# Storing fifteen partitions of two chunks by Pool's software queue, and 112 of the others by the hardware queue

## The chip, the core and the metric

The kernel runs on one core of a Trainium2 chip. The metric is device time in microseconds (us), lower is better; a run of before and of a variant share a chip, and only runs of the fast state are compared. Two variants did not always run on one chip; on every chip used, before took 164.6 to 164.9 us (medians), and where two variants are compared the ratios to before agree with the difference quoted. A profile is one execution, with times counted from the start of its span; its span is about 1.8 us shorter than the device time of the same execution.

## The reference

```python
x_flat = x.reshape(-1, 256)                    # 32768 x 256, fp32
y = x_flat @ W + scale * (((x_flat @ lora_A) * lora_E) @ lora_B)
```

The output is 32768 x 256 in fp32. So 33.6 MB come in and 33.6 MB go out, and the weights are small: `W + A diag(E) B` is folded into one 256 x 256 matrix on the chip.

## The kernel before

The rows are cut into eight chunks of 4096. In a chunk, partition p holds 32 consecutive rows of 256 floats, a *line* of 32 KB that is contiguous in DRAM too. Six "homes" in SBUF (the on-chip memory of 128 partitions) hold chunks; a chunk is loaded, multiplied, its result written over its input, and stored from there. All DMAs are issued by SP on one hardware queue.

```python
ORDER = ["L0", "L1", "L2", "L3", "L4", "L5",
         "S0", "S1", "L6", "L7", "S2", "S3", "S4", "S5", "S6", "S7"]
...
x_chunks = x_flat.rearrange("(c p b) k -> c p b k", p=P, b=ROWS)   # P = 128, ROWS = 32
y_chunks = out_flat.rearrange("(c p b) m -> c p b m", p=P, b=ROWS)
homes = [sbuf(f"home{h}", [P, ROWS, K], FP32) for h in range(N_HOMES)]
...
    else:                                       # a store, in SP's program
        sync.wait_ge(s_chunk, c + 1)
        sync.dma_start(out=y_chunks[c], in_=home(c)[:]).then_inc(...)
...
# the last store stands after the five engines' programs have ended
nc.sync.dma_start(out=y_chunks[last], in_=home(last)[:])
```

Pool (GpSimd) casts x to bf16, TensorE transposes and multiplies, ScalarE and VectorE move results out of PSUM. Pool's program ends with its casts.

## Time and profile before

| | before |
|---|---|
| time, median of 4 runs | 164.65 us (164.32 to 165.16) |
| span of the profile | 163.2 us |
| DMA, mean over the span | 413 GB/s |
| busiest compute engine | PE, 60% |
| last eviction ends (timeline) | 121.8 us |

The slices view cuts the span in 40 equal parts (4.08 us each). Its DMA row is the mean busy share of 16 DMA engines in tenths, and GB/s is what they moved. The queue table gives for each queue its packets, MB and share of 16 engines' span. The windows view gives for a stretch the busy time of each engine, the granted clock, the DMA share and GB/s.

```profile
PE   0399938999999999999920099999950000000000
DMA  5999998998998999999999999999999999999980
GB/s 163 412 458 454 393 506 385 426 474 385 466 434 385 498 401 387 393 474 420 418 466 393 442 450 393 468 426 418 450 418 426 458 401 458 442 401 466 418 385 16
q1 hardware_dynamic: 2944, 67.41, 96.7%
```

The DMA row stands at 8 or 9 tenths from the second slice to the last but one, while the PE row is empty in the last ten slices. The kernel is bound by its DMA engines, and at the end by stores alone.

The trace also has each DMA packet with its start, duration and size, and each engine's completion increment. A 32 KB line is one packet and takes 1213 ns. Followed back from the last increment, the late engine moves eight such lines in each of the last four stores. The sixteen increments of the last store land at 159.30 us (first), 160.08 us (fifteenth) and 162.26 us (sixteenth): one engine is 2.2 us late. Its lines took mostly 1274 to 1300 ns while stores ran beside compute, and 1213 ns in loads and after compute had ended. Its number the trace does not give, and its cause is open.

### The profile page before, as it was taken

The numbers are of one execution on the slowest core, as the hardware profiler recorded it, in microseconds if no ns is written. First come the engines' busy times: TensorE is split into PE (matmuls) and PEld (weight loads), VectorE is DVE, ScalarE is ACT, GpSimd is POOL, SyncE is SP. The second block draws the span as 40 slices with busy tenths as digits, with TensorE's granted clock in tenths as the row PEclk, the third lists the DMA queues.
The fourth block names the chain that finished last, engine by engine and source line by source line (L and its number), as shares of the span: only waits on it lengthen the run. The fifth ranks groups of instructions, "written<-read, shape, count | busy, mean of one in ns | idle before, by whom it ended". The sixth has DMA issues, their size and how long they took to land. (4 is left out here: it accounts for less than half of the span.)

```text
span 163.2 us, 2145 instructions
## 1 busy us (share of the span) xinstructions
PE 98.3 (60%) x778; PEld 81.7 (50%) x778; DVE 79.5 (49%) x66; ACT 66.1 (40%) x65; POOL 67.1 (41%) x70
## 2 busy tenths in 40 slices
PE   0399938999999999999920099999950000000000
PEld 0268827888888888888810078888840000000000
DVE  0116961888888888888850026888870000000000
ACT  3045723767777676767720026676720000000000
POOL 1445516767777677777400256677400000000000
PEclk9999996999999999999995558999995555555555
DMA  5999998998998999999999999999999999999980
GB/s 163 412 458 454 393 506 385 426 474 385 466 434 385 498 401 387 393 474 420 418 466 393 442 450 393 468 426 418 450 418 426 458 401 458 442 401 466 418 385 16
DMA packets 2948, 67.43 MB, mean 413 GB/s; under 512 B 497, under 2 KB 513, under 8 KB 641
## 3 DMA queue, kind: packets, MB, share of 16 engines
q1 hardware_dynamic: 2944, 67.41, 96.7%
q14 instruction: 4, 0.02, 0.0%
HBM read 33.85 MB, written 33.55 MB: 413 GB/s over the span
## 5 line engine op out<-in xcount | busy, mean ns | idle before, releaser
L171 DVE COPY home<-psum_y 128x1024 f32<-128x1024 f32 x64 | 78.4, 1225 | 32.3 <-PE psum_y L192 29.6
L141 POOL CAST stage<-home 128x1024 bf16<-128x1024 f32 x64 | 66.4, 1041 | 48.3 <-DMA home<-in_x_dram 24.5
L152 ACT COPY xt<-psum_xt 128x1024 bf16<-128x1024 bf16 x64 | 64.8, 1012 | 52.2 <-PE psum_xt L184 52.2
L192 PE MATMUL psum_y<-weff,xt 128*128 128x256 bf16 x512 | 69.8, 281 | 0.9
L192 PEld LDWEIGHTS psum_y<-weff,xt 128*128 128x128 bf16 x512 | 47.9, 101 | 14.6 <-issue 7.1
L184 PE MATMUL psum_xt<-ident,stage 128*128 128x128 f32 x260 | 42.0, 287 | 14.5 <-PEq L177 14.5
L184 PEld LDWEIGHTS psum_xt<-ident,stage 128*128 128x128 f32 x260 | 32.7, 149 | 16.6 <-issue 15.6
L204 PE MATMUL psum_y<-ident,a_sb 128*16 128x128 f32 x2 | 0.6, 394 | 6.8 <-DMA a_sb<-in_lora_A_dram 6.8
L157 DVE TENSOR_SCALAR ate<-psum_y,e_sb 16x256 f32<-16x256 f32 x1 | 0.5, 471 | 7.5 <-PE psum_y L204 7.5
L204 PEld LDWEIGHTS psum_y<-ident,a_sb 128*16 128x16 f32 x2 | 0.1, 90 | 6.8 <-issue 6.8
L210 PE MATMUL psum_y<-b_sb,ate 16*128 16x256 f32 x4 | 2.1, 670 | 0.0
L167 DVE TENSOR_TENSOR weff<-w_sb,psum_y 128x512 bf16<-128x512 f32 x1 | 0.7, 689 | 2.4 <-PE psum_y L210 2.4
L152 ACT ACT_TABLE_LOAD x1 | 1.3, 1283 | 0.9 <-SPq L218 0.9
L210 PEld LDWEIGHTS psum_y<-b_sb,ate 16*128 16x128 f32 x4 | 1.2, 319 | 0.5 <-issue 0.3
L123 POOL MEMSET ident<- 128x128 f32 x1 | 0.2, 205 | 0.5 <-SPq L218 0.5
L125 POOL TENSOR_SCALAR_AFFINE_SELECT ident<-ident 128x128 f32<-128x128 f32 x1 | 0.3, 293 | 0.2 <-POOL ident L123 0.2
L246 POOL MEMSET const-float32-0.0<- 128x1 f32 x1 | 0.1, 98 | 0.2 <-issue 0.2
L246 POOL MEMSET const-bfloat16-1.0<- 128x1 bf16 x1 | 0.1, 101 | 0.0
L246 POOL MEMSET const-uint8-127<- 128x1 uint8 x1 | 0.1, 101 | 0.0
L246 POOL MEMSET const-float32-1.0<- 128x1 f32 x1 | 0.1, 98 | 0.0
## 6 DMA issues: line engine op xcount, KB each, us to landing
out_dram<-home SPq DMA_DIRECT2D x8, 4096.0 KB, 42.4
home<-in_x_dram SPq DMA_DIRECT2D x7, 4096.0 KB, 28.5
home<-in_x_dram SPq DMA_DIRECT2D x2, 1024.0 KB, 5.2
home<-in_x_dram SPq DMA_DIRECT2D x1, 2048.0 KB, 10.0
w_sb<-in_W_dram SPq DMA_DIRECT2D x1, 256.0 KB, 5.1
a_sb<-in_lora_A_dram SPq DMA_DIRECT2D x1, 16.0 KB, 4.8
e_sb<-in_lora_E_dram SPq DMA_DIRECT2D x1, 0.1 KB, 4.5
b_sb<-in_lora_B_dram SPq DMA_DIRECT2D x1, 16.0 KB, 3.9
```

The source lines that it names most:

```text
L123: gpsimd.memset(ident[:], 0.0).then_inc(s_ident, 1)
L125: gpsimd.affine_select(out=ident[:], in_=ident[:], compare_op=ALU.not_equal, fill=1.0, base=0, pattern=[[-1, P]], channel_multiplier=1,).t ...
L141: gpsimd.tensor_copy(out=stage[g % NS][:], in_=home(c)[:, b:b + CG, :]).then_inc(s_stage, 1)
L152: scalar.copy(out=xt[g % NX][:], in_=halves).then_inc(s_xt, 1)
L157: vector.tensor_scalar(out=ate[:], in0=psum_y[0][:R, :KT, :P], scalar1=e_sb[:], scalar2=float(scale), op0=ALU.mult, op1=ALU.mult,).then_in ...
L167: vector.tensor_add(out=weff[:], in0=w_sb[:], in1=psum_y[1][:, :KT, :]).then_inc(s_free, NY)
L171: vector.tensor_copy(out=home(c)[:, b:b + CG, :], in_=psum_y[g % NY][:]).then_inc(s_free, 1)
L184: ins = tensor.transpose(psum_xt[i % NT][:, b, :], words[:, b, :], ident[:])
L192: ins = tensor.matmul(psum_y[i % NY][:, b, :], xt[i % NX][:, b, t, :], weff[:, t, :], start=(t == 0), stop=(t == KT - 1),)
L204: ins = tensor.transpose(psum_y[0][:R, t, :P], a_sb[:, t, :], ident[:])
L210: ins = tensor.matmul(psum_y[1][:, t, :], ate[:, t, :], b_sb[:], start=True, stop=True)
L246: nc = _bacc.Bacc("TRN2", target_bir_lowering=False, num_devices=1)
```

## The change

The intent is to give one DMA engine two lines fewer. In chunks 4 and 5, partitions 0 to 111 stay on the hardware queue (by division, seven lines for each of 16 engines). Partitions 112 to 126 send 31 of their 32 rows, for both chunks, by Pool's software queue: fifteen shares of two lines, meant for fifteen engines. Before them, a DMA of five partitions goes out on the same queue; it is meant to turn the choice of engines so that the fifteen leave out the late one. Row 31 of these partitions and all of partition 127 go in small DMAs.

```diff
+PAIR = (4, 5)
+SKIPPED = 4
+COMMON = 112
-    homes = [sbuf(f"home{h}", [P, ROWS, K], FP32) for h in range(N_HOMES)]
+    homes = sbuf("homes", [P, N_HOMES, ROWS, K], FP32)
...
-                sync.dma_start(out=y_chunks[c], in_=home(c)[:]).then_inc(...)
+                if c not in PAIR:
+                    parts = [(slice(P), slice(ROWS))]
+                else:
+                    parts = [
+                        (slice(COMMON + SKIPPED + 1, P - 1), slice(ROWS - 1, ROWS)),
+                        (slice(P - 1, P), slice(0, ROWS, 2)),
+                        (slice(P - 1, P), slice(1, ROWS, 2)),
+                        (slice(COMMON), slice(ROWS)),
+                    ]
+                for i, (p, b) in enumerate(parts):
+                    sync.dma_start(out=y_chunks[c, p, b], in_=home(c)[p, b]).then_inc(...)
...
+        gpsimd.wait_ge(s_chunk, PAIR[1] + 1)      # after Pool's last cast
+        for p, b in (
+            (slice(COMMON, COMMON + SKIPPED + 1), slice(ROWS - 1, ROWS)),
+            (slice(COMMON, P - 1), slice(ROWS - 1)),
+        ):
+            gpsimd.dma_start(out=y_pair[p, :, b], in_=home_pair[p, :, b]).then_inc(s_pair, 16)
+        gpsimd.wait_ge(s_pair, 32)
+        for s in s_rows:
+            gpsimd.wait_ge(s, 16)
```

More of the change, by code (lines that the diff above doesn't have):

```diff
@@ L90 @@
     s_chunk = sem("chunk_done")
+    s_pair = sem("pair_stored")
+    s_rows = [sem(f"rows_stored_{c}") for c in PAIR]
     def home(c):
-        return homes[c % N_HOMES]
+        return homes[:, c % N_HOMES]
     sync, gpsimd, scalar, vector, tensor = nc.sync, nc.gpsimd, nc.scalar, nc.vector, nc.tensor
@@ L119, in sync_program @@
                 sync.wait_ge(s_chunk, c + 1)
-                sync.dma_start(out=y_chunks[c], in_=home(c)[:]).then_inc(stored_of.get(c, stored_rest), 16)
+                if c not in PAIR:
[8 more added lines that the diff above has]
+                for i, (p, b) in enumerate(parts):
+                    done = s_rows[PAIR.index(c)] if len(parts) > 1 and i == 0 else stored_of.get(c, stored_rest)
+                    sync.dma_start(out=y_chunks[c, p, b], in_=home(c)[p, b]).then_inc(done, 16)
     def gpsimd_program():
@@ L144, in gpsimd_program @@
         gpsimd.drain().then_inc(s_stage, 1)
+        gpsimd.wait_ge(s_chunk, PAIR[1] + 1)
+        y_pair = y_chunks[PAIR[0]:PAIR[1] + 1].rearrange("c p b m -> p c b m")
+        home_pair = homes[:, PAIR[0]:PAIR[1] + 1]
+        for p, b in (
[6 more added lines that the diff above has]
+            gpsimd.wait_ge(s, 16)
     def scalar_program():
@@ L228 @@
     last = int(ORDER[-1][1:])
-    nc.sync.dma_start(out=y_chunks[last], in_=home(last)[:])
+    nc.sync.dma_start(out=y_chunks[last], in_=home(last))
 _INS = ['x', 'W', 'lora_A', 'lora_B', 'lora_E', 'scale']
```

## The prediction

> **What bounds the kernel now.** The 16 DMA engines. In the slices view the DMA row stands at 9 tenths from the fourth slice or so to the end, and the queue table gives one hardware queue 96.7% of 16 engines' span (413 GB/s, 163.2 us). No compute engine is over 60% busy; the last eviction ends at 121.8 us, and the last 40 us are stores alone. In the trace's packets a 32 KB line takes 1213 ns; each engine moves 120 (145.6 us) and some smaller ones.
>
> **The uneven end.** The last store's completion increments land at 159.3 to 160.1 us from fifteen engines and at 162.26 us from one. The kernel waits 2.2 us for it alone. Following that engine's packets backwards: its lines took 1274 to 1300 ns between 63 and 82.7 us and between 105 and 120 us, and one took 1865 ns at 100.9 us. There stores run beside compute; in loads, and in stores after compute, it runs at 1213 ns. The trace does not number the engines, so I can't see which it is.
>
> **What the change does.** Chunks 4 and 5 were 16 lines of 32 KB on every engine. Now partitions 0 to 111 go by the hardware queue (14 lines per engine), and partitions 112 to 126 by Pool's queue, two 31 KB lines on each of fifteen engines. Leftover 1 KB rows go in small DMAs. [...]
>
> Costs per engine, with a 1 KB packet at 46 ns and a completion write at 9 ns (trace), and a 31 KB line at 1175 ns (estimate from 1213):
> - fifteen engines: 2 x (1175 - 1213) = -76, 1 KB packets +184 to +276, completions about +75: +0.2 to +0.3 us;
> - the one left out: -2426 + about 350 = -2.1 us.
>
> If that is the late one, it comes in at about 160.2 us, the others at about 160.3: the last landing moves from 162.26 to about 160.4, all on the critical path. Pool's casts end near 118 us, before its DMAs; at S7's issue (122.2 us) three chunks are still queued[...]. Compute and the first 90 us are unchanged.
>
> **Prediction.** 162.9 us (-1.1%), 162.1 to 165.2 in 8 cases of 10. Chances: faster by over 2% 0.04, within 2% 0.92, slower by over 2% 0.04. The floor is near 162.5 us, since the balanced engines still need their 160.
>
> **What would show it.** Right: span near 161.3 us; the last increments within about 1 us; a second queue with about 0.95 MB; total bytes unchanged; the lines of 1274 to 1300 ns still on one engine, which has two lines fewer. Wrong engine: one ends early, near 158 us, and the late one stays, at about 162.5 (time 164.9).
>
> **What would make it wrong.** [...]fifteen partitions are spread otherwise; the slow engine changes between runs or chips; the slowness belongs to the profile; [...]Pool's wait[...] lengthens the end.

+0.2 to +0.3 us for fifteen engines and -2.1 us for the one left out put the last landing at 160.4 us instead of 162.26, and the time at 162.9 us. That the one left out is the late one was assumed. SP's issues take 0.33 to 0.70 us each in the profile before, and three chunks are queued when the last store is issued; that they hide behind the queue was an estimate.

## The result

The changed kernel takes 180.83 us (median of 4 runs, 180.06 to 181.49) against 164.65 us. The ratio is 1.0978, interval 1.0924 to 1.1032: slower by 16 us. Ratios here are the mean time of one kernel's fast runs over that of the other's of the same rounds, so not quite the ratio of the medians quoted.

The slices and the queue table of the changed kernel (a slice is now 4.49 us):

```profile
PE   0499849999999999997009999980000000000000
DMA  5998999999899998998999999999999998999510
GB/s 190 434 485 372 452 467 416 401 467 445 372 467 467 350 432 387 461 459 387 438 459 423 403 452 430 423 424 424 194 256 313 307 285 321 394 438 408 219 73 15
q1 hardware_dynamic: 3080, 66.44, 90.2%
q0 software_dynamic: 80, 0.96, 3.5%
```

The MB are the same in sum (67.4). Compute ends at the same time, as the last two evictions show (VectorE's timeline, before and then after):

```profile
119.20 2.58 DVE L171 COPY home<-psum_y 128x1024 f32<-128x1024 f32 x2 [0.24 <-PE psum_y L192]
```

```profile
119.17 2.58 DVE L204 COPY homes<-psum_y 128x1024 f32<-128x1024 f32 x2 [0.24 <-PE psum_y L225]
```

The DMA row still says 9 tenths, yet from the 29th slice (126 us) the same busy engines move 194 to 321 GB/s instead of some 430. The windows view, before and then after:

```profile
core 0: us, PE busy (x) PEld busy (x) DVE busy (x) ACT busy (x) POOL busy (x), PEclk, DMA share, GB/s
120.00:150.00 30.00, 0.51 (x5) 0.20 (x3) 1.65 (x2) 0.00 (x0) 0.00 (x0) 0.55 1.01 435
```

```profile
120.00:150.00 30.00, 0.49 (x5) 0.19 (x2) 1.62 (x2) 0.00 (x0) 0.00 (x0) 0.55 1.00 296
```

The engines were as busy (1.00) and moved 296 GB/s instead of 435. So nothing waits for a command: the packets themselves take longer. From the packets that start after 115 us:

```
                  32 KB lines: n, mean ns, longest    31 KB lines: n, mean ns, longest
before            578   1213   1293                   -
after             548   1395   5179                   30   3281   8114
```

This accounts for the loss. The 548 lines took 182 ns too long on average, 100 us of engine time; the 30 software lines 2106 ns too long against my estimate of 1175, 63 us. Together that is 163 us on 16 engines, 10.2 us each. The mean of the last store's sixteen increments moved by 10.4 us, from 159.82 to 170.23. The rest is unevenness: the last increment came 8.5 us after that mean (178.74 us), before 2.4 us after it. 10.4 + 6.1 is the 16.5 us between the two last increments.

What the prediction assumed, that the engine left out is the late one, did come true. The trace does not number engines, but on one engine each packet starts 3 to 4 ns before the one ahead of it ends, so an engine can be followed where its packets are alone. Four of the sixteen in the changed kernel, from 104 to 135 us:

```
mean ns of its 32 KB lines    31 KB lines    2 KB packets of the software queue
(104.5 to 119 us)
1213                          2              1
1213                          2              0
1289                          0              1
1213                          2              1
```

The engine with the slow lines is the one that got no 31 KB line. It got a packet of the five-partition DMA. The same holds in three later variants (e5, e11, e14). The right engine was relieved. By what rule the queue chooses its engines no run shows.

One other thing is new: SP waits for Pool before it issues the last store (SP's waits, then SP's timeline, of the changed kernel).

```profile
SPq L251 <- POOLq L251: 19.3, 1, 19.3
```

```profile
141.41 0.35 SPq L262 DMA_DIRECT2D out_dram<-homes  x1
```

### The profile page after: what moved, and what is told of

Read it like the earlier page. It is cut to its first block, busy times and chain, and to the rows that moved or that the text cites. A ratio compares the mean times of both kernels' runs of the same rounds, so it can differ in the third digit from the quotient of the medians.

```text
span 179.7 us, 2155 instructions
## 1 busy us (share of the span) xinstructions
PE 100.6 (56%) x778; PEld 82.7 (46%) x778; DVE 79.5 (44%) x66; ACT 66.1 (37%) x65; POOL 68.3 (38%) x72
## 5 line engine op out<-in xcount | busy, mean ns | idle before, releaser
L204 DVE COPY homes<-psum_y 128x1024 f32<-128x1024 f32 x64 | 78.4, 1225 | 32.2 <-PE psum_y L225 30.2
L163 POOL CAST stage<-homes 128x1024 bf16<-128x1024 f32 x64 | 66.4, 1040 | 48.3 <-PE psum_xt L217 27.0
L225 PE MATMUL psum_y<-weff,xt 128*128 128x256 bf16 x512 | 70.7, 284 | 0.2
L217 PE MATMUL psum_xt<-ident,stage 128*128 128x128 f32 x260 | 42.8, 291 | 12.8 <-PEq L210 12.8
L217 PEld LDWEIGHTS psum_xt<-ident,stage 128*128 128x128 f32 x260 | 33.3, 152 | 15.0 <-issue 14.0
L174 POOL DMA_DIRECT2D out_dram<-homes x2 | 1.2, 626 | 1.2 <-PE psum_xt L217 1.2
```

The lines of the kernel that those rows point to most:

```text
L163: gpsimd.tensor_copy(out=stage[g % NS][:], in_=home(c)[:, b:b + CG, :]).then_inc(s_stage, 1)
L174: gpsimd.dma_start(out=y_pair[p, :, b], in_=home_pair[p, :, b]).then_inc(s_pair, 16)
L204: vector.tensor_copy(out=home(c)[:, b:b + CG, :], in_=psum_y[g % NY][:]).then_inc(s_free, 1)
L217: ins = tensor.transpose(psum_xt[i % NT][:, b, :], words[:, b, :], ident[:])
L225: ins = tensor.matmul(psum_y[i % NY][:, b, :], xt[i % NX][:, b, t, :], weff[:, t, :], start=(t == 0), stop=(t == KT - 1),)
```

## The experiments

**The theories.** *Partitions*: how long a line takes depends on which partitions are read at the same time, not on its size alone. In before's trace every store after 115 us has all 128 partitions, and a 32 KB line takes 1213 ns there, 27.0 GB/s. The change departs from that form twice: the software shares read partitions 112 to 126 alone, and two stores have 112 partitions instead of 128. This was a supposition, to be tested by runs that differ in partitions. The recorded expectations call it theory 1 or the ports theory, after a mechanism; what they say of the mechanism, and the model made from it, is cut, since no run shows it and the trace numbers neither engines nor partitions. The times that they expect stand as estimates. *Rivals*: the software queue, by itself or beside the other queue; SP's late issue of the last store; the small DMAs.

### Same bytes, other partitions: e7 and e8

Both change one line of the kernel before: chunks 4 and 5 store 64 partitions only, by division four lines for each of 16 engines. Half of those chunks stays unstored.

```diff
-                sync.dma_start(out=y_chunks[c], in_=home(c)[:]).then_inc(...)
+                p = slice(32, 96) if c in (4, 5) else slice(P)     # e8: slice(0, 64)
+                sync.dma_start(out=y_chunks[c, p], in_=home(c)[p]).then_inc(...)
```

> The kernel before, but the stores of chunks 4 and 5 carry partitions 32 to 95 alone (a wrong result on purpose: half of those two chunks is not stored), all by the hardware queue, four lines on each of 16 engines. [...]Ports theory: 8 lines per engine fewer, 9.7 us less: about 155 us, lines at 1213 ns.

> The same with partitions 0 to 63: same bytes, same shapes, same lines per engine[...]. Ports theory: lines of these two stores take 2 x 1213 ns and the half chunks take as long as whole ones: 162 to 166 us. If [...]128 partitions are special for another reason, both runs give the same time.

Partitions 32 to 95 gave 155.17 us, partitions 0 to 63 gave 164.13 us. The DMAs have the same shape, count, queue and bytes. The windows view, e7 and then e8:

```profile
120.00:150.00 30.00, 0.00 (x0) 0.00 (x0) 1.19 (x1) 0.00 (x0) 0.00 (x0) 0.54 0.97 419
```

```profile
120.00:150.00 30.00, 0.58 (x6) 0.27 (x3) 1.71 (x2) 0.00 (x0) 0.00 (x0) 0.55 0.99 291
```

In the packets, e7's lines take 1213 ns. Those of e8 take 2514 to 2549 ns on average in each 4 us between 124 and 136 us: twice as long and 4 to 5% more. Leaving out half of the two chunks gained 9.6 us in e7 and 0.7 us in e8 (before took 164.80 us beside them): read from partitions 0 to 63 alone, half of the lines cost nearly as much time as all of them. Which engine reads which partition the trace does not show. The two runs also write other DRAM rows; e4 and e5 below do not differ in that.

### The two parts, each by itself: e1, e2, e4, e5

e1 is the changed kernel with Pool's two DMAs issued by SP. Pool's waits stay.

```diff
-            gpsimd.dma_start(out=y_pair[p, :, b], in_=home_pair[p, :, b]).then_inc(s_pair, 16)
+                        sync.dma_start(out=y_pair[p, :, b], in_=home_pair[p, :, b]).then_inc(s_pair, 16)   # after chunk 5's parts
```

> The changed kernel, with the two DMAs of partitions 112 to 126 issued by SP's hardware queue instead of Pool's software queue; Pool still waits for them, so the queue is the only difference. Theory 1 (ports): [...]expected 175 to 183 us, and lines of 31 KB still taking 2 to 4 us instead of 1.2. Rival (the software queue itself[...]): back to about 165 us, 31 KB lines at 1.2 us.

It took 182.69 us, ratio 1.1096. Its thirty 31 KB lines took 4535 ns on average. The software queue is not needed for the loss: the same shares by the hardware queue are no faster. But the queue was not the only difference, as the expectation had it: followed through its packets, the engine with the slow lines (1288 ns) got a 31 KB line in e1, so it was not left out.

e2 stores only partitions 0 to 111 of chunks 4 and 5, with no software DMA and no small ones (wrong).

> Stores of chunks 4 and 5 carry partitions 0 to 111 alone, seven lines on each engine; nothing stores the other sixteen partitions (a wrong result on purpose, 1 MB less traffic), and Pool stores nothing. If the hardware DMA of 112 partitions is as good as one of 128, the end comes 2 lines per engine earlier, 2.4 us: about 162.2 us. Theory 1 says it is not: [...]about 168 to 172 us.

It took 176.53 us (fast runs 176.01 to 176.74, ratio 1.0707), with 1 MB less to move. The direction is the partitions theory's, the size is not: my estimate, from the model that is cut, was 168 to 172 us. In the trace (of a run in the slow state) 71 lines took over half as long again as 1213 ns. One engine was alone at the end: fifteen increments by 166.64 us, the sixteenth at 176.64; twelve of its fourteen lines in these two stores took 1.5 to 2.7 times as long, 2.48 us on average, near the 2.51 to 2.55 us of e8's lines. As far as its packets can be followed back, it is the engine with the slow lines before compute ends. What the model had wrong I can't tell, since the trace shows neither engine numbers nor partitions.

e4 and e5 take the software part alone. The kernel before stays whole, with 128-partition stores, and Pool copies two 31 KB lines of fifteen partitions to a scratch tensor, 0.95 MB more.

```diff
+        gpsimd.dma_start(out=extra[0:5, :, 0:1], in_=homes[112:117, 4:6, 31:32]).then_inc(s_first, 16)
+        gpsimd.wait_ge(s_first, 16)
+        gpsimd.dma_start(out=extra, in_=homes[112:127:1, 4:6, 0:31]).then_inc(s_pair, 16)   # e4
+        gpsimd.dma_start(out=extra, in_=homes[36:93:4, 4:6, 0:31]).then_inc(s_pair, 16)     # e5, instead
```

> The kernel before, all stores of 128 partitions, and on top Pool's queue copies two 31 KB lines of each of partitions 112 to 126 to a scratch tensor: the software part of the change by itself, as 0.95 MB more traffic. Two lines more on fifteen engines cost 2.4 us if nothing meets: about 167 us. Theory 1: [...]172 to 178 us, 31 KB lines at 2 to 5 us.

> As the run before it, but the fifteen partitions are 36, 40, ... 92[...]. Same queue, same bytes[...]. Theory 1: mostly gone, 166 to 170 us[...]. If the software queue itself is slow, it is as slow as the run before it.

e4 took 175.75 us, e5 166.28 us. Only the fifteen partitions differ. The issue table (KB each, us from issue to landing), e4 and then e5:

```profile
extra<-homes POOLq DMA_DIRECT2D x1, 930.0 KB, 20.0
```

```profile
extra<-homes POOLq DMA_DIRECT2D x1, 930.0 KB, 10.8
```

The mean software line took 4535 ns from partitions 112 to 126 and 1237 ns from 36, 40, ... 92. So each part alone costs over 9 us, and the two queues side by side cost next to nothing: of e5's thirty software lines only one took over half as long again as 1175 ns, and e5 took 1.5 us more than before (164.74 us) with 0.95 MB more to move.

### The rivals: e3 and e6

e3 is the kernel before with chunks 4 and 5 stored whole by Pool's software queue.

```diff
+                if c in (4, 5):                       # in SP's program
+                    continue
...
+        for c in (4, 5):                              # in Pool's, where the change has its DMAs
+            gpsimd.dma_start(out=y_chunks[c], in_=home(c)[:]).then_inc(s_pair, 16)
+        gpsimd.wait_ge(s_pair, 32)
```

> The kernel before with the whole stores of chunks 4 and 5 (128 partitions, 32 KB lines[...]) issued by Pool's software queue when the change issues its own DMAs, and Pool waiting for them at the end as in the change. If the software queue or the alternation of two queues costs, this shows it on 8 MB instead of 1 MB: over 175 us if it were the cause of the 16 us. Ports theory: within 1 us of before, 164 to 166 us, lines of both queues near 1213 ns.

It took 166.94 us, ratio 1.0135, 1 us above what I had allowed. 8.4 MB went by the software queue with lines at 1213 ns. The 2 us come from elsewhere, as the slices and SP's timeline show:

```profile
DMA  5999999989989898999999999899999999993885
GB/s 175 427 427 447 502 391 391 502 383 463 431 383 510 383 385 383 471 425 399 486 391 455 431 407 486 385 431 463 391 486 399 431 455 399 479 407 136 383 383 255
```

```profile
152.29 0.33 SPq L236 DMA_DIRECT2D out_dram<-home  x1
```

That the late issue costs the 2 us is read from this one trace, not tested. SP issues the last store at 152.29 us, after Pool has waited for its DMAs, but by then both queues had run dry: the 37th slice moves 136 GB/s. In the changed kernel that issue comes at 141.41 us, and no such hole is in its slices.

e6 moves that last store into SP's own program, so that it does not wait for Pool.

```diff
-        for step in ORDER[:-1]:
+        for step in ORDER:
...
+        sync.wait_ge(stored_of[N_CHUNKS - 1], 16)
```

> The changed kernel, but the last store (chunk 7) is issued in SP's own program when its chunk is done, not after Pool has finished waiting (141.4 us in the changed kernel's profile, where SP waits 19.3 us for Pool). If that late issue cost anything on the critical path, this is faster than 180.8 by up to the delay; since the hardware queue still holds chunk 6 at 141 us, expected the same, 179 to 182 us.

Its four runs took 181.69 to 185.97 us; only the fastest is fast, so no interval can be given. That one, 181.69 us, is not faster than the change's 180.83. So the late issue is not the cause, as far as one fast run shows.

### Both repairs with the change's own bytes: e9 to e12

e9 is the control to e2: again 3584 KB for each of the two chunks, but as 28 rows of 128 partitions (wrong).

```diff
+                b = slice(0, 28) if c in (4, 5) else slice(ROWS)
+                sync.dma_start(out=y_chunks[c, :, b], in_=home(c)[:, b]).then_inc(...)
```

> The control to the run with partitions 0 to 111 alone (176.5 us): the stores of chunks 4 and 5 carry 28 of 32 rows of all 128 partitions, again 3584 KB each and 1 MB less in all (wrong result on purpose)[...]. Ports theory: 2.4 us under before, 161.5 to 163.5 us. If 3584 KB or the missing rows were the reason for 176.5, it is as slow.

162.50 us, against 176.53 us for the same bytes as 112 partitions. The windows view of e2 and then of e9:

```profile
120.00:150.00 30.00, 0.11 (x2) 0.00 (x0) 1.23 (x1) 0.00 (x0) 0.00 (x0) 0.59 0.99 344
```

```profile
120.00:150.00 30.00, 0.59 (x6) 0.29 (x3) 1.73 (x2) 0.00 (x0) 0.00 (x0) 0.56 1.01 436
```

The other three are the changed kernel with one or both repairs. "Spread" lets the software shares read partitions 36, 40, ... 92; "28 rows" replaces the 112 partitions by 28 rows of 128, and then the software and the small DMAs write to a scratch tensor, since their rows would be written twice. All three give wrong values; DMA counts, queues and bytes are the change's.

```diff
-            gpsimd.dma_start(out=y_pair[p, :, b], in_=home_pair[p, :, b]).then_inc(s_pair, 16)
+            src = p if b == slice(ROWS - 1, ROWS) else slice(36, 93, 4)                      # e10, e11
+            gpsimd.dma_start(out=y_pair[p, :, b], in_=home_pair[src, :, b]).then_inc(s_pair, 16)
-                        (slice(COMMON), slice(ROWS)),
+                        (slice(P), slice(ROWS - 4)),                                         # e11, e12
```

> The changed kernel, the fifteen software shares reading partitions 36, 40, ... 92[...] instead of 112 to 126[...], to the same DRAM addresses (values wrong on purpose): nothing else differs. The hardware stores still carry 112 partitions. Ports theory: the part of the loss that the software lines make goes, the part of the 112 partitions stays: 174 to 180 us, 31 KB lines mostly near 1.2 to 2.4 us.

> Both repairs: the hardware stores of chunks 4 and 5 carry 28 rows of all 128 partitions (the same 3584 KB), the software shares[...] and the small DMAs write to a scratch tensor (wrong result on purpose, since rows 28 to 31 of the two chunks are not stored). Queues, DMA counts, bytes and lines per engine are those of the change[...]. This is what the prediction costed: 162.9 us, range 162 to 164.5. If something else of the change costs, it stays above 165.

> As the run before it, with the software shares back on partitions 112 to 126[...]. Ports theory: 171 to 176 us (the extra copy[...] was 175.7 with 1 MB more).

| time, us (ratio to before) | shares from partitions 112 to 126 | shares from 36, 40, ... 92 |
|---|---|---|
| 112 partitions | 180.83 (1.0978), the change | 177.66 and 178.74, the fast runs (1.0804), e10 |
| 28 rows of 128 | 171.68 (1.0408), e12 | 165.05 (1.0010), e11 |

Both repairs together take away 15.8 us. Each takes away less while the other departure is still there: with the 112 partitions in place, spreading the shares gains about 3 us; with 28 rows it gains 6.6. The larger part is the 112 partitions. The windows view of e12 and then of e11:

```profile
120.00:150.00 30.00, 0.00 (x0) 0.00 (x0) 1.16 (x1) 0.00 (x0) 0.00 (x0) 0.53 1.00 348
```

```profile
120.00:150.00 30.00, 0.00 (x0) 0.00 (x0) 1.03 (x1) 0.00 (x0) 0.00 (x0) 0.58 1.00 427
```

But e11 is a miss for the prediction: I expected 162 to 164.5 us, and 165.05 is no gain on before at all. So one step was still open: is relieving the late engine worth nothing?

### What was left: e13, e14, e15

By the model, which no run shows, a few of e11's shares should still be slow. e13 gives the shares other partitions, in a DMA of eleven and one of four:

```diff
+            (slice(112, 117), slice(112, 117), slice(31, 32)),      # 5 shares
+            (slice(112, 123), slice(52, 93, 4), slice(31)),         # 11 shares
+            (slice(123, 127), slice(32, 45, 4), slice(31)),         # 4 shares
```

> As the run with both repairs (128 partitions of 28 rows[...], 165.05 us), but the fifteen shares are issued as eleven and four[...] (wrong result on purpose). [...]this gives 162 to 163.3 us with all of the last increments within about 1 us[...]. If it stays at 165, something other than ports holds it.

The 162 to 163.3 us were expected if those few shares were what held e11 back.

> As the run with both repairs, without the six small DMAs of SP (partition 127 in 16 pieces of 1 KB, twice per chunk, and the row of ten partitions). 84 KB less are worth 0.2 us by bytes. If the small DMAs are what keeps the repaired form at 165.05, this gives about 163[...].

e13 took 164.98 us, a miss: no better than e11, although its software lines took 1176 ns on average (longest 1211). Its sixteen last increments end at 160.82 us (fifteenth) and 162.19 us (sixteenth), so one engine is late, but it is another one. Followed by their packets, the engine with the slow lines has no 31 KB line and is among the others (its last packet ends at 159.6 us): it was relieved. The late one has two 31 KB lines, and lost 1.9 us in two store lines of 1492 and 2638 ns, which started at 119.5 and 130.0 us and lasted into the two bursts of the small DMAs' 1 KB packets (from 120.2 and 131.2 us). e14 is e11 without SP's six small DMAs: 163.52 us (ratio 0.9917, interval 0.9895 to 0.994). They carry 84 KB, 0.2 us by bytes at the 413 GB/s of before's profile, and their absence gains 1.5 us.

e15 is e13 without the small DMAs.

> [...] (165.0 us with the small DMAs) and without the six small DMAs. [...]So 162.4 to 163.3 us, what the prediction asked for the change. If it stays above 164, the late engine is not relieved by two lines fewer.

163.06 us, ratio 0.9895 (0.9869 to 0.9921). The last increments land at 159.34 (first), 160.12 (fifteenth) and 160.55 us (sixteenth). All software lines took 1175 ns, all 28-row lines at most 1095 ns, where e13 had one of 2638.

So the small DMAs cost 1.9 us in this form, where the prediction's line for them came to some 0.3 us. Why they do is not shown; e13's two slow lines overlap their bursts. What the small DMAs cost in the change itself, beside its larger losses, no run shows.

e15 is not a kernel: rows 28 to 31 of two chunks are not stored. I found no correct version that beats before, and ran none. The 1% of e15 is the most that relieving the late engine gained in any run here with nearly the change's bytes; how much of it a correct version could keep is not shown.

## Why the prediction was wrong

- *What bounds the kernel, and the late engine*: right. The DMA engines bound it, and the late one is late in e9 too (157.77 and 159.58 us).
- *The choice of engine*: right, but by luck as far as the prediction goes. It said that it couldn't see which engine is late, and 162.9 us took for granted that the change leaves out that one. The slow engine got no 31 KB line.
- *Hidden issue costs*: right for the change, as far as e6's one fast run shows. e3 shows the limit: when the queues run dry before Pool's wait ends, it costs about 2 us.
- *Relief worth 1.9 us*: right in size, once nothing else was in the way. e15 has its last increment at 160.55 us, where the prediction said 160.4, and takes 163.06 us, where it said 162.9. (It moves 84 KB less.)
- **The step that failed** is the cost line "fifteen engines: 2 x (1175 - 1213) = -76, ... +0.2 to +0.3 us". It costs a line by its size alone, at 1213 ns for 32 KB, whatever partitions are read. The runs showed in its place 3281 ns for a 31 KB line and 1395 ns for the 32 KB lines beside and behind it, 10.4 us on the mean engine and 6.1 us more on the last. "14 lines per engine" for the 112 partitions failed too: that part alone is worth 14 us (176.53 us in e2 against 162.50 in e9). The small DMAs' term of the same line is mis-sized too where it could be measured: 1.9 us (e13 against e15). What it is in the change itself no run shows.
- Of the things that "would make the prediction wrong" I listed the spread over *engines*, and not the partitions that they read. Before's late stores all have 128 partitions, so its 1213 ns say nothing of 112 or of fifteen, and I didn't ask.

## What to carry to other kernels

An equal number of lines on each engine is worth little if the partitions are chosen badly: with the same lines and bytes, a line took 1213 ns from partitions 32 to 95 and 2514 to 2549 ns from partitions 0 to 63 (e7, e8). In a kernel that keeps all engines busy, try first to store all 128 partitions and cut by rows (loads were not tested), not by partitions: 162.50 against 176.53 us here (e9, e2). Where a few partitions must go alone, measure which: fifteen took 1237 ns a line from 36, 40, ... 92 and 4535 ns from 112 to 126 (e5, e4). When the DMA row says 9 tenths and GB/s falls, look at the duration of one packet.
